# Shifted places in SBUF for activations and split weights of a decoder step, with one ring skipped per MLP chunk

## The chip, the cores and the metric

The kernel runs on one core of one Trainium2 chip. The metric is the time of one execution on the device, in microseconds (us): the median of three runs of the kernel before was 2753.49 us (2752.89 to 2754.78). The profile is of one further execution.

## The reference

The reference is one inference step of a two-layer decoder on 320 tokens: 256 of a prompt and 8 x 8 of samples. Width is 2048. Layer 0 mixes tokens by gated linear attention (four heads, chunks of 64, a carried state), layer 1 by a gated MLP over positions (chunks of 128). Each layer ends with a dense MLP of inner width 8192. Residuals are scaled and normalised:

```python
def sq_relu_mlp(x, w1, w2):
    return jnp.square(jax.nn.relu(x @ w1)) @ w2
...
h, s = gla_mixer(x, ...)          # layer 0;  sg_mixer(x, ...) in layer 1
x = layer_norm(DEEPNORM_ALPHA * x + h, ln1_g[i], ln1_b[i])
x = layer_norm(DEEPNORM_ALPHA * x + sq_relu_mlp(x, mlp_w1[i], mlp_w2[i]), ln2_g[i], ln2_b[i])
```

All inputs and outputs are float32. The outputs are both groups' activations, both new attention states, and the normalised v rows of layer 1.

## The kernel before, in words

Activations are kept transposed: 128 features on the partitions, 16 k tiles of T = 320 tokens along the free dimension, so one k tile is 1,280 bytes in each partition. Weights are the stationary operand, activations stream. To keep float32 accuracy with the faster fp32r type, every operand is split into a high part, rounded to fp32r, and a low part, the rest. `mm3` (lines 149 to 154) makes one product of three matmuls into the same PSUM tile: low weights with high activations (line 152), high weights with low activations (153), high with high (154). They are 17,664 of the kernel's matmuls.

Weights come in units (`unit`, lines 130 to 143): four k tiles by 256 output columns. A unit is a DMA of 512 KB from the SP queue into one of three `raw` buffers, a cast on ScalarE into the high tile (line 141) and a subtraction on VectorE into the low tile (line 142). TensorE then does 24 matmuls on it: two column halves, four k tiles, three products. `group` (line 156) walks over the four units (q = 0 to 3) of one block of 256 output columns, so the k tile is 4 q plus the tile in the unit; `gemm`, `gemm_of` and `residual_gemm` walk over the blocks. A GEMM of 2048 x 2048 is 32 units or 768 matmuls.

High and low tiles stand in rings (`Ring`, lines 47 to 58). A ring has two buffers of 4,096 bytes for the high part, a gap, two for the low part, and a second gap that fills up to 256 bytes (LINE = 64 floats). High tiles start at a multiple of 256 bytes; low tiles lie the gap beyond one. `next_ring` takes the rings in turn: "a" and "c" from the start, in the attention; "b" and "d" as well, once `second_half` (line 625) has freed space, during the output projection of layer 0. So from there on the four units of a group always meet the same four rings in the same order.

Activation tiles have a spare of 64 floats (BIG, line 35), and `bigtile` (line 189) may begin inside it. PLACES (line 37) gives these starts, in floats, for the high and low part, for each MLP: four pairs for the hidden tiles (hh, hl) of the four chunks of the MLP, one for its input y (yh, yl), and one for other tiles (the input of `sg_w_in` from the first row, ph and pl, the input of `sg_w_out`, from the second). The tiles of x, o and dg begin at 0. dg is the residual before its normalisation, with two further columns (TW = 322): the first group of a GEMM reads it while the normalisation is still being worked out, and `correct` mends the result.

An MLP (`mlp`, line 799) goes in four chunks of 2048 inner columns. Each is a w1 GEMM, whose results are squared and split into hh and hl on their way out of PSUM (lines 811 to 813), and a w2 GEMM, whose results are added to z. The order on each engine comes from the tile framework's planner, which follows the order of the program text and the readiness of operands; TensorE's order is that of the loops above.

Of the kernel before, what the change touches and what calls it, by code (L numbers as in the profile page):

```python
# [20 lines left out]
T = TP + DB * DS  # L21
# [12 lines left out]
LINE = 64  # L34
BIG = KT * T + LINE

PLACES = [[(0, 0), (16, 16), (32, 32), (48, 48), (0, 16), (16, 32)],
          [(32, 48), (48, 0), (0, 48), (16, 0), (32, 16), (48, 32)]]


V_BG, V_NG = 0, 8
# [5 lines left out]
class Ring:  # L47
# [5 lines left out]
    def part(self, p, name):  # L53

        t = self.pool.tile([P, UK, UN], F32R, tag=p + self.tag, name=name)
        if self.gap:
            self.pool.tile([P, self.gap.pop(0)], F32, tag=f"gap{p}{self.tag}", name=name + "_gap", bufs=1)
        return t


class Side:
# [17 lines left out]
def step_kernel(ctx: ExitStack, tc: tile.TileContext, A):  # L79
# [3 lines left out]
    def nm(s):  # L83
        uid[0] += 1
        return f"{s}_{uid[0]}"
# [5 lines left out]
    wa = ctx.enter_context(tc.tile_pool(name="wa", bufs=2))  # L91
# [2 lines left out]
    gl = gls.enter_context(tc.tile_pool(name="gl", bufs=4, space=bass.MemoryType.PSUM))  # L94
    mx = None

    rings = [Ring(wa, "a", 32), Ring(wa, "c", 48)]
    turn = [0]
    banks = [0]
    units = [0]  # L100
# [25 lines left out]
    def col(c):  # L126
        return vec[:, c : c + 1]
# [17 lines left out]
    def next_ring():  # L145
        turn[0] += 1
        return rings[turn[0] % len(rings)]
# [38 lines left out]
    w_in = A["gla_w_in"]  # L186
    C_Q, C_K, C_V, C_R = 0, H * DK, 2 * H * DK, 2 * H * DK + H * DV

    def bigtile(tag, dt, name, width=T, start=0):

        t = (lp if tag == "b1" else big).tile([P, BIG], dt, tag=tag, name=nm(name))
        return t[:, start : start + KT * width].rearrange("p (k t) -> p k t", t=width)

    def parts(pair, name, width=T, starts=(0, 0)):
        return (bigtile(pair + "0", F32R, name + "h", width, starts[0]),
                bigtile(pair + "1", F32R, name + "l", width, starts[1]))

    xh, xl = parts("a", "x")
    o_all = bigtile("b0", F32, "o_all")

    gst = ExitStack()
# [104 lines left out]
    class Head:  # L306


        def __init__(hd, h):
            hd.h = h  # L310
            hd.eb, hd.ei, hd.ee = {}, {}, {}
# [304 lines left out]


    oh, ol = parts("a", "o")

    def split_o(ks):  # L620
        for k in ks:
            nc.scalar.copy(oh[:, k, 0:T], o_all[:, k, 0:T])
            nc.vector.tensor_sub(ol[:, k, 0:T], o_all[:, k, 0:T], oh[:, k, 0:T].bitcast(F32))

    def second_half():

        nonlocal lp, l2, z, gl, mx
        side.flush()
        split_o(range(4 * (H - 1), 4 * H))
        gst.close()  # L630
        gls.close()
        gl = ctx.enter_context(tc.tile_pool(name="gs", bufs=2, space=bass.MemoryType.PSUM))
        mx = ctx.enter_context(tc.tile_pool(name="mx", bufs=2, space=bass.MemoryType.PSUM))
        banks[0] = 3
        lp = ctx.enter_context(tc.tile_pool(name="lp", bufs=1))
        l2 = ctx.enter_context(tc.tile_pool(name="l2", bufs=2))
        wb = ctx.enter_context(tc.tile_pool(name="wb", bufs=2))
        rings.extend((Ring(wb, "b", 8), Ring(wb, "d", 40)))
        wb.tile([P, LINE // 4], F32, tag="fill", name="fill_b", bufs=1)
        z = lp.tile([P, KT, T], F32, tag="z", name="z")  # L640
        lp.tile([P, LINE], F32, tag="fill", name="fill_l")
        for q in range(2):
            nc.gpsimd.dma_start(z[:, 8 * q : 8 * q + 8, :], xT[:, 8 * q : 8 * q + 8, :])
# [113 lines left out]
    def gemm(w, row0, col0, rh, rl, evict, quad=False, side=None, before=None):  # L757

        i = 0
        while i < D // UN:  # L760
            n2 = 2 if quad and i == 0 else 1
            group(w, row0, [col0 + (i + m) * UN for m in range(n2)], rh, rl,
                  lambda n, ps, i=i: evict(2 * i + n, ps), side, before=before if i == 0 else None)
            i += n2

    def gemm_of(norm, out, w, col0, evict_raw, evict, starts):

        yh, yl = parts(out, "y", starts=starts)
        norm.close()
        side = Side([lambda j=j: norm.apply(j, yh, yl) for j in range(KT)], 3 * NU)  # L770
        group(w, 0, (col0, col0 + UN), *norm.raw, evict_raw, side, width=TW)
        side.flush()
        for i in range(2, D // UN):
            group(w, 0, (col0 + i * UN,), yh, yl, lambda n, ps, i=i: evict(2 * i + n, ps))
        return yh, yl

    def residual_gemm(w, rh, rl, row0, scale, vg, vb, raw, quad=False, side=None, before=None, last=False):

        norm = None

        def evict(j, ps):
            nonlocal norm
            if j == 0:
                norm = Norm(z, vg, vb, raw, last)
            zj = z[:, j, :]
            if j < KT // 2:
                nc.vector.scalar_tensor_tensor(zj, zj, scale, ps[:], op0=ALU.mult, op1=ALU.add)
            else:
                nc.vector.tensor_add(zj, zj, ps[:])
            norm.add(j)  # L790
            if j == KT // 2 - 1:
                for i in range(KT // 2, KT):
                    zi = z[:, i, :]
                    nc.vector.scalar_tensor_tensor(zi, zi, scale, norm.c[:], op0=ALU.mult, op1=ALU.subtract)

        gemm(w, row0, 0, rh, rl, evict, quad, side, before)
        return norm

    def mlp(i, norm, y_in, h_in, vg, vb, raw, last=False):

        w1, w2 = A["mlp_w1"][i], A["mlp_w2"][i]
        NC_ = 4
        for c in range(NC_):
            hs = []

            def sq_relu(j, x, r):
                if not hs:
                    hs.extend(parts(h_in, "h", starts=PLACES[i][c]))
                hh, hl = hs
                f = l2.tile([P, T], F32, tag="f", name=nm("f"))  # L810
                nc.vector.scalar_tensor_tensor(f[:], x, 0.0, r[:], op0=ALU.max, op1=ALU.mult)
                nc.scalar.copy(hh[:, j, 0:T], f[:])
                nc.vector.tensor_sub(hl[:, j, 0:T], f[:], hh[:, j, 0:T].bitcast(F32))

            def evict(j, ps):
                r = l2.tile([P, T], F32, tag="r", name=nm("r"))
                nc.scalar.activation(r[:], ps[:], AF.Relu)
                sq_relu(j, ps[:], r)

            def evict_raw(j, ps):  # L820
                t, wb_ = norm.correct(ps)
                r = l2.tile([P, T], F32, tag="r", name=nm("r"))
                nc.scalar.activation(r[:], t[:], AF.Relu, bias=wb_)
                sq_relu(j, r[:], r)

            if c == 0:
                yh, yl = gemm_of(norm, y_in, w1, 0, evict_raw, evict, PLACES[i][4])
            else:
                gemm(w1, 0, c * D, yh, yl, evict)
            if c < NC_ - 1:  # L830
                def evz(j, ps, s=ALPHA if c == 0 else 1.0):
                    nc.vector.scalar_tensor_tensor(z[:, j, :], z[:, j, :], s, ps[:], op0=ALU.mult, op1=ALU.add)
                gemm(w2, c * D, 0, *hs, evz)
            else:
                return residual_gemm(w2, *hs, c * D, 1.0, vg, vb, raw, last=last)
# [4 lines left out]
    def before(q):  # L840
        if q == NU - 1:
            second_half()

    norm = residual_gemm(A["gla_w_out"], oh, ol, 0, ALPHA, V_L1G, V_L1B, "b", quad=True,
                         side=side, before=before)
    norm = mlp(0, norm, "a", "b", V_L2G, V_L2B, "a")


# [21 lines left out]
    def put_v(j, x, bias):  # L870
        nonlocal v, nv
        if j == 0:
            v = bigtile("a0", F32, "v")
            nv = Norm(v, V_SG, V_SBB)
        vj = v[:, j, 0:T]
        nc.scalar.activation(vj, x, AF.Gelu, bias=bias)
        if j >= KT // 2:
            nc.vector.tensor_sub(vj, vj, nv.c[:])
        nv.add(j)
        if j == 3:  # L880
            spatial()

    def ev_v_raw(j, ps):
# [5 lines left out]
    yh, yl = gemm_of(norm, "b", A["sg_w_in"], D, ev_v_raw, lambda j, ps: put_v(j, ps[:], col(V_SB + KT + j)),  # L889
                     PLACES[0][5])  # L890

# [43 lines left out]
    gemm(A["sg_w_in"], 0, 0, yh, yl, ev_u, side=side)  # L935
    ph, pl = parts("b", "p", starts=PLACES[1][5])
    for k in range(KT):
        nc.scalar.copy(ph[:, k, 0:T], v[:, k, 0:T])
        nc.vector.tensor_sub(pl[:, k, 0:T], v[:, k, 0:T], ph[:, k, 0:T].bitcast(F32))

    norm = residual_gemm(A["sg_w_out"], ph, pl, 0, ALPHA, V_L1G + KT, V_L1B + KT, "a", quad=True)
    norm = mlp(1, norm, "b", "a", V_L2G + KT, V_L2B + KT, "b", last=True)


# [20 lines left out]
    for j in range(KT):  # L965
        y, g, b = z[:, j, :], col(norm.vg + j), col(norm.vb + j)
        if j in on_pool:
            t = l2.tile([P, T], F32, tag="s", name=nm("t"))
# [3 lines left out]
        else:  # L972
            if j not in ps:
                put_d(j)
            t = l2.tile([P, T], F32, tag="t", name=nm("t"), bufs=3)
# [70 lines left out]
```

## Time and profile before

| What | Value |
|---|---|
| Median of the runs (lowest, highest) | 2753.49 us (2752.89, 2754.78) |
| The profiled execution's own time | 2754.99 us |
| Its span, first to last instruction | 2753.3 us |
| Mean granted TensorE clock | 0.998 |
| HBM read, written | 409.60 MB, 22.02 MB |
| DMA over the span | 157 GB/s |

The span lies 1.7 us below the execution's own time. In the page, PE is TensorE's matmuls, PEld its weight loads, DVE VectorE, ACT ScalarE, POOL GpSimd, SP the engine that issues most DMAs; "busy" is the time in which at least one instruction of the engine runs. A matmul's recorded duration runs from its start to its modelled end and overlaps the next one's, so a mean of 309 ns doesn't mean that one begins every 309 ns. In a row of a group, "x768 | 242.5, 316 | 10.1" is the count, the busy time in us, the mean duration in ns and the idle time of the engine before them. In a row of a stretch, the count in brackets takes in all instructions that overlap the stretch.

### The profile page before, as it was taken

The numbers are of one execution on the slowest core, as the hardware profiler recorded it, in microseconds if no ns is written. First come the engines' busy times: TensorE is split into PE (matmuls) and PEld (weight loads), VectorE is DVE, ScalarE is ACT, GpSimd is POOL, SyncE is SP. The second block draws the span as 40 slices with busy tenths as digits, with TensorE's granted clock in tenths as the row PEclk, the third lists the DMA queues.
The fourth block names the chain that finished last, engine by engine and source line by source line (L and its number), as shares of the span: only waits on it lengthen the run. The fifth ranks groups of instructions, "written<-read, shape, count | busy, mean of one in ns | idle before, by whom it ended". The sixth has DMA issues, their size and how long they took to land.

```text
span 2753.3 us, 44617 instructions
## 1 busy us (share of the span) xinstructions
PE 2728.7 (99%) x18493; PEld 2705.0 (98%) x18493; DVE 1546.0 (56%) x2284; ACT 1185.3 (43%) x1698; POOL 54.6 (2%) x84
## 2 busy tenths in 40 slices
PE   8999999999999999999999999999999999999998
PEld 8999998999999999999999999999999999999998
DVE  6567577785444444444468764686444444444446
ACT  5545455464334334333446554455334323323434
POOL 1000000000000000000001000000000000000001
PEclk9999999999999999999999999999999999999999
DMA  6557566645444444444445444454444444444442
GB/s 223 178 194 233 174 201 207 199 140 160 149 150 152 148 152 147 152 149 150 151 142 169 153 138 131 138 159 152 150 151 148 153 147 152 149 150 148 151 147 75
DMA packets 126396, 434.52 MB, mean 158 GB/s; under 512 B 13681, under 2 KB 17905, under 8 KB 126193
## 3 DMA queue, kind: packets, MB, share of 16 engines
q1 hardware_dynamic: 118800, 407.29, 47.5%
q0 software_dynamic: 6512, 23.20, 2.5%
q8 instruction: 144, 2.36, 0.3%
q10 hardware_dynamic: 880, 1.18, 0.1%
q14 instruction: 60, 0.48, 0.0%
HBM read 409.60 MB, written 22.02 MB: 157 GB/s over the span
## 4 chain that ended last, share of the span: by engine, by line
PE 97%; DVE 1%; DMA 1%; ACT 1%; issue 0%; SPq 0%; ACTq 0%; DVEq 0%
PE mm L154 31%; PE mm L152 31%; PE mm L153 31%; PE gl L564 1%; PE gl L567 1%; PE gl L522 0%; PE gl L905 0%; PE gl L506 0%; DMA xr<-xT 0%; DMA raw<-gla_w_out 0%; DMA raw<-gla_w_in 0%; ACT z L979 0%; PE gl L900 0%; ACT wh L141 0%; DVE wl L142 0%
## 5 line engine op out<-in xcount | busy, mean ns | idle before, releaser
L142 DVE TENSOR_TENSOR wl<-raw,wh 128x1024 fp32r<-128x1024 f32 (+1 forms) x738 | 901.9, 1223 | 967.3 <-ACT wh L141 964.6
L141 ACT CAST wh<-raw 128x1024 fp32r<-128x1024 f32 (+1 forms) x738 | 773.4, 1049 | 1234.6 <-PE mm L154 1124.6
L154 PE MATMUL mm<-yh,wh 128*128 128x320 f32 x2368 | 731.9, 310 | 0.0
L153 PE MATMUL mm<-yl,wh 128*128 128x320 f32 x2368 | 730.5, 309 | 0.0
L152 PE MATMUL mm<-yh,wl 128*128 128x320 f32 x2368 | 726.3, 309 | 0.0
L154 PE MATMUL mm<-hh,wh 128*128 128x320 f32 x2048 | 632.5, 309 | 0.0
L153 PE MATMUL mm<-hl,wh 128*128 128x320 f32 x2048 | 632.4, 309 | 0.0
L152 PE MATMUL mm<-hh,wl 128*128 128x320 f32 x2048 | 631.4, 308 | 0.0
L154 PEld LDWEIGHTS mm<-yh,wh 128*128 128x128 f32 x2368 | 445.2, 188 | 0.0
L153 PEld LDWEIGHTS mm<-yl,wh 128*128 128x128 f32 x2368 | 444.8, 188 | 0.0
L152 PEld LDWEIGHTS mm<-yh,wl 128*128 128x128 f32 x2368 | 443.6, 188 | 0.0
L153 PEld LDWEIGHTS mm<-hl,wh 128*128 128x128 f32 x2048 | 384.8, 188 | 0.0
L152 PEld LDWEIGHTS mm<-hh,wl 128*128 128x128 f32 x2048 | 384.5, 188 | 0.0
L154 PEld LDWEIGHTS mm<-hh,wh 128*128 128x128 f32 x2048 | 384.4, 188 | 0.0
L152 PE MATMUL mm<-xh,wl 128*128 128x320 f32 x768 | 242.5, 316 | 10.1 <-ACT xh L215 5.6
L153 PE MATMUL mm<-xl,wh 128*128 128x320 f32 x768 | 238.7, 311 | 0.0
L154 PE MATMUL mm<-xh,wh 128*128 128x320 f32 x768 | 238.6, 311 | 0.0
L152 PEld LDWEIGHTS mm<-xh,wl 128*128 128x128 f32 x768 | 145.5, 190 | 15.0 <-ACT xh L215 5.6
L153 PEld LDWEIGHTS mm<-xl,wh 128*128 128x128 f32 x768 | 145.7, 190 | 3.6 <-issue 1.2
L154 PEld LDWEIGHTS mm<-xh,wh 128*128 128x128 f32 x768 | 145.6, 190 | 1.3
L152 PE MATMUL mm<-oh,wl 128*128 128x320 f32 x256 | 79.2, 313 | 4.8 <-DVE nw L178 4.8
L153 PE MATMUL mm<-ol,wh 128*128 128x320 f32 x256 | 79.8, 313 | 0.0
(271 smaller groups left out, 2475.4 us busy)
## 6 DMA issues: line engine op xcount, KB each, us to landing
raw<-mlp_w SPq DMA_DIRECT2D x512, 512.0 KB, 3.5
raw<-gla_w_in SPq DMA_DIRECT2D x94, 512.0 KB, 3.9
raw<-sg_w_in SPq DMA_DIRECT2D x64, 512.0 KB, 3.6
st<-state SPq DMA_DIRECT2D x32, 512.0 KB, 4.1
o_state_s<-st POOLq DMA_DIRECT2D x32, 512.0 KB, 3.9
raw<-gla_w_out SPq DMA_DIRECT2D x32, 512.0 KB, 4.1
raw<-sg_w_out SPq DMA_DIRECT2D x32, 512.0 KB, 3.5
z<-xT POOLq DMA_DIRECT2D x2, 1280.0 KB, 10.5
```

The lines of the kernel that those rows point to most:

```text
L141: nc.scalar.copy(hi[:, ks, :], raw[:, ks, :])
L142: nc.vector.tensor_sub(lo[:, ks, :], raw[:, ks, :], hi[:, ks, :].bitcast(F32))
L152: nc.tensor.matmul(ps, wl[:, kk, s], x_h, start=first, stop=False)
L153: nc.tensor.matmul(ps, wh[:, kk, s], x_l, start=False, stop=False)
L154: nc.tensor.matmul(ps, wh[:, kk, s], x_h, start=False, stop=last)
L564: nc.tensor.matmul(po[:], qm[:, kt, b * P : (b + 1) * P], part[:], start=False, stop=(b == DB - 1 and kt == 1 and part is sth))
L567: nc.tensor.matmul(pu[:], kz[:, g, i, kt * P : (kt + 1) * P], hd.vts[:, g, :], start=True, stop=True)
```

## The change

Three things change, all of them addresses or the choice of a buffer.

1. Hidden, y and p tiles are reached through a new class `Rows`. Tile k begins at `start + k*T + 4*(k//2)` floats: every second tile, the offset grows by 16 bytes, to 112 bytes at the last two. The high and low part do so alike. Tiles without a start in PLACES (x, o, dg, v) are as before.
2. PLACES: hidden tiles of all four chunks start at 0 and 0 in the first MLP, at 32 and 32 floats in the second. Starts of y and of the input of `sg_w_in` stay; p goes from (48, 32) to (32, 0).
3. The gap between high and low weights becomes 16, 24, 32 and 8 floats in rings a, c, b and d (64, 96, 128 and 32 bytes; before 128, 192, 32 and 160). At each MLP chunk `next_ring()` is called once more, so one ring is passed over, and units meet the rings shifted by one.

```diff
-PLACES = [[(0, 0), (16, 16), (32, 32), (48, 48), (0, 16), (16, 32)],
-          [(32, 48), (48, 0), (0, 48), (16, 0), (32, 16), (48, 32)]]
+PLACES = [[(0, 0)] * 4 + [(0, 16), (16, 32)], [(32, 32)] * 4 + [(32, 16), (32, 0)]]
...
+class Rows:
+    def __init__(self, buf, start):
+        self.buf, self.start = buf, start
+
+    def __getitem__(self, key):
+        p, k, t = key
+        at = self.start + k * T + 4 * (k // 2)
+        return self.buf[p, at + t.start : at + t.stop]
...
-    rings = [Ring(wa, "a", 32), Ring(wa, "c", 48)]
+    rings = [Ring(wa, "a", 16), Ring(wa, "c", 24)]
...
-    def bigtile(tag, dt, name, width=T, start=0):
+    def bigtile(tag, dt, name, width=T, start=None):
 
         t = (lp if tag == "b1" else big).tile([P, BIG], dt, tag=tag, name=nm(name))
+        if start is not None:
+            return Rows(t, start)
+        start = 0
         return t[:, start : start + KT * width].rearrange("p (k t) -> p k t", t=width)
 
-    def parts(pair, name, width=T, starts=(0, 0)):
+    def parts(pair, name, width=T, starts=(None, None)):
...
-        rings.extend((Ring(wb, "b", 8), Ring(wb, "d", 40)))
+        rings.extend((Ring(wb, "b", 32), Ring(wb, "d", 8)))
...
         for c in range(NC_):
             hs = []
+            next_ring()
```

## The prediction

> **What bounds the kernel now.** I read the page's busy times first, then the chain that ended last, then the costliest groups.
>
> ```profile
> PE 2728.7 (99%) x18493; PEld 2705.0 (98%) x18493; DVE 1546.0 (56%) x2284; ACT 1185.3 (43%) x1698; POOL 54.6 (2%) x84
> ...
> PE 97%; DVE 1%; DMA 1%; ACT 1%; issue 0%; SPq 0%; ACTq 0%; DVEq 0%
> PE mm L154 31%; PE mm L152 31%; PE mm L153 31%; PE gl L564 1%; PE gl L567 1%; PE gl L522 0%; PE gl L905 0%; PE gl L506 0%; DMA xr<-xT 0%; DMA raw<-gla_w_out 0%; DMA raw<-gla_w_in 0%; ACT z L979 0%; PE gl L900 0%; ACT wh L141 0%; DVE wl L142 0%
> ...
> L142 DVE TENSOR_TENSOR wl<-raw,wh 128x1024 fp32r<-128x1024 f32 (+1 forms) x738 | 901.9, 1223 | 967.3 <-ACT wh L141 964.6
> L141 ACT CAST wh<-raw 128x1024 fp32r<-128x1024 f32 (+1 forms) x738 | 773.4, 1049 | 1234.6 <-PE mm L154 1124.6
> ...
> raw<-mlp_w SPq DMA_DIRECT2D x512, 512.0 KB, 3.5
> ```
>
> TensorE never stops: the three matmuls of mm3 (lines 152 to 154) are 93% of the chain. Casting and splitting the weights is not late; ACT sits idle 1124.6 us before its casts because TensorE has not yet given a weight buffer back. So only the pitch of the matmuls (start to start) counts. 736 units of 24 matmuls make 17,664 of them, so 1 ns of pitch is 17.7 us.
>
> A matmul's duration overlaps the next one's. The timeline shows the pitch, and what runs beside it.
>
> ```profile
> 1000.05 0.30 PE L152 MATMUL mm<-hh,wl 128*128 128x320 f32 x1
> 1000.05 0.19 PEld L153 LDWEIGHTS mm<-hl,wh 128*128 128x128 f32 x1
> 1000.19 0.31 PE L153 MATMUL mm<-hl,wh 128*128 128x320 f32 x1
> 1000.19 0.19 PEld L154 LDWEIGHTS mm<-hh,wh 128*128 128x128 f32 x1
> ```
>
> The load of the next weights begins with each matmul and reads SBUF while the activations stream. Where these two reads lie to each other is all that the change touches, so I ask whether the pitch depends on place. Below are stretches of 110 us, each inside one GEMM of 768 equal matmuls: time, then each engine's busy time with its instruction count. First the four w2 GEMMs of the first MLP (hh, hl), then four of the second, then three w1 GEMMs of the first MLP (yh, yl), three of the second, last sg_w_out (ph, pl).
>
> ```profile
> core 0: us, PE busy (x) PEld busy (x) DVE busy (x) ACT busy (x) POOL busy (x), PEclk, DMA share, GB/s
> ...
> 686.00:796.00 110.00, 110.00 (x754) 110.00 (x753) 45.45 (x49) 34.27 (x34) 0.00 (x0) 1.00 0.49 151
> 912.00:1022.00 110.00, 110.00 (x757) 110.00 (x756) 46.09 (x49) 33.41 (x33) 0.00 (x0) 1.00 0.49 152
> 1137.00:1247.00 110.00, 110.00 (x752) 110.00 (x751) 45.60 (x47) 33.18 (x33) 0.00 (x0) 1.00 0.49 151
> 1362.00:1472.00 110.00, 110.00 (x753) 110.00 (x752) 71.52 (x113) 46.34 (x63) 0.00 (x0) 1.00 0.48 151
> 1944.00:2054.00 110.00, 110.00 (x752) 110.00 (x751) 45.30 (x48) 34.23 (x34) 0.00 (x0) 1.00 0.47 150
> 2170.00:2280.00 110.00, 110.00 (x757) 110.00 (x756) 46.04 (x48) 33.76 (x33) 0.00 (x0) 1.00 0.49 152
> 2395.00:2505.00 110.00, 110.00 (x746) 110.00 (x745) 44.64 (x47) 33.32 (x33) 0.00 (x0) 1.00 0.48 149
> 2621.00:2731.00 110.00, 110.00 (x748) 110.00 (x747) 64.12 (x106) 38.55 (x58) 0.00 (x0) 1.00 0.36 110
> ...
> 800.00:910.00 110.00, 110.00 (x751) 110.00 (x750) 51.71 (x61) 44.17 (x60) 0.00 (x0) 1.00 0.49 149
> 1025.00:1135.00 110.00, 110.00 (x750) 110.00 (x750) 51.70 (x61) 44.18 (x60) 0.00 (x0) 1.00 0.47 149
> 1250.00:1360.00 110.00, 110.00 (x751) 110.00 (x751) 51.68 (x61) 44.15 (x60) 0.00 (x0) 1.00 0.48 150
> 2057.00:2167.00 110.00, 110.00 (x752) 110.00 (x751) 51.23 (x61) 44.33 (x60) 0.00 (x0) 1.00 0.48 151
> 2283.00:2393.00 110.00, 110.00 (x752) 110.00 (x751) 51.81 (x61) 44.11 (x60) 0.00 (x0) 1.00 0.49 149
> 2508.00:2618.00 110.00, 110.00 (x752) 110.00 (x751) 51.23 (x61) 44.34 (x60) 0.00 (x0) 1.00 0.48 151
> ...
> 1719.00:1829.00 110.00, 110.00 (x750) 110.00 (x749) 75.83 (x123) 49.62 (x74) 0.00 (x0) 1.00 0.48 149
> ```
>
> About two matmuls of each count were begun before the stretch, so the pitch is 110.00 over the count less 2. The clock is 1.00 throughout and TensorE full, yet the GEMMs differ: 145.7 ns (x757) to 147.8 ns (x746). Rows with equal places repeat within one matmul (the w1 rows). So place matters, by about 2 ns between best and worst.
>
> **What the change does to each stage.** By stage, with L the distance of low weights behind high ones modulo 256 bytes, and h and l the offsets of the activations' two parts:
>
> Second-half stages now use L = 128, 192, 32 and 160 in turn; afterwards 64, 96, 128 and 32. Tiles of 1,280 bytes keep one offset modulo 256 through a GEMM now; afterwards it moves by 16 bytes every second k tile, from 0 to 112 over sixteen tiles. The first MLP's hidden tiles start at h = l = 0, 64, 128, 192 in its four chunks, later always at 0. The second MLP's start at (128, 192), (192, 0), (0, 192), (64, 0), later always at (128, 128). The y tiles keep their starts; p goes from (192, 128) to (128, 0). No matmul, load or byte is added.
>
> The nearest row for a moving offset is the normalised activations dg, whose tiles are 322 columns wide, so that each k tile lies 8 bytes further modulo 256, with h = l.
>
> ```profile
> L152 PE MATMUL mm<-dgh,wl x64: 304/310/316, 572.2 to 600.7; 128*128 128x322 f32 x64
> ```
>
> From first to last are 63 triples and four statistics matmuls (lines 679 and 680): 28.5 us / 193 = 147.7 ns, and by 320/322 for the wider tile 146.8 ns. A moving offset thus gives neither the best nor the worst row but the middle, and starts off every 32-byte border cost nothing to speak of. I take 146.8 ns for every stage that moves. The ends are the best and worst row, 145.7 and 147.8.
>
> The sum, from the pitches in the rows:
> - First MLP, w2: 3,072 matmuls, rows 754, 757, 752, 753, mean 110/752 = 146.3. To 146.8: +1.6 us. This stage loses, because equal fixed offsets do better than the middle.
> - Second MLP, w2: 3,072, rows 752, 757, 746, 748, mean 110/748.75 = 146.9: -0.3 us.
> - w1, first MLP: 2,880 at 110/748.67 = 146.9: -0.4 us. Second: 2,880 at 110/750 = 146.7: +0.4 us. sg_w_in: 1,344, whose offsets keep their starts too, taken at 146.8: 0.
> - sg_w_out: 768 at 110/748 = 147.1: -0.2 us.
> - The first half, where the x tiles don't move but L does (rings a and c, 128 and 192 to 64 and 96):
>
> ```profile
> 174.70:186.70 12.00, 12.00 (x85) 12.00 (x84) 4.69 (x6) 5.09 (x9) 0.00 (x0) 1.00 0.49 156
> ...
> 174.58 0.31 PE L153 MATMUL mm<-xl,wh 128*128 128x320 f32 x1
> ...
> 186.67 0.30 PE L152 MATMUL mm<-xh,wl 128*128 128x320 f32 x1
> ```
>
> From 174.58 to 186.67 lie 83 matmuls (85 less 2): 145.7 ns, as good as the best row. This place is given up for two that no row shows. 2,304 matmuls, and some 384 of gla_w_out before the other rings open: nothing if the new pair is as good, +1.1 ns or 3.0 us if it is middling, +2.1 ns or 5.6 us if it is as the worst row. I take half of the middling loss, +1.5 us, as equal zero offsets did well in the row x754 too.
> - dg itself: 576 matmuls, new L only, taken at 0; between best and worst row ±0.6 us.
> - Evictions that now write at 16-byte offsets: no such write is in the trace but dg's; the casts and subtractions of h are these.
>
> ```profile
> L813 DVE TENSOR_TENSOR hl<-f,hh 128x320 fp32r<-128x320 f32 x128 | 62.5, 488 | 29.5 <-ACT hh L812 29.5
> L812 ACT CAST hh<-f 128x320 fp32r<-128x320 f32 x128 | 58.8, 459 | 32.4 <-DVE f L811 32.4
> ```
>
> They lie beside matmuls on engines 56% and 43% busy; doubled, they would still be hidden: 0.
> - The skipped ring at each chunk's start: four rings of two buffers give some seven units of 3.5 us (24 x 146.8 ns) ahead, six or so after a skip. Load 3.5, cast 1.0 and subtraction 1.2 us fit in: 0. Without that cover the eight skips would cost 5.7 us each, 46 us.
>
> Together +2.6 us. The profiled execution took 2754.99 us (span 2753.3 and 1.7 around it) and so comes to 2757.6; the median shown is 1.5 us lower, so I predict **2756 us**. Bounds of the moving stages: 14,016 matmuls at the best row's 145.7 instead of 146.7 are -14 us, at the worst row's 147.8 +15 us; an average over sixteen meetings of q and L per stage should stay well inside, at a third of that.
>
> **The rivals.** (1) *The new places are good.* For it: the rows x757 (twice) and the x stage show 145.7 is to be had, and hidden tiles with h = l do better than unequal ones (146.3 against 146.9). Against: dg moves with h = l and is middling. If the moving stages reach 145.7 throughout, -14 us: 2739; halfway with the x stage unchanged, 2747.
>
> (2) *Slower: the moving offset keeps meeting badly.* If each shift sets the two reads to collide anew, before the stream has settled, the moving stages go towards the row x746, +1.1 ns on 14,016: +15 us, and with the first half's loss of 3.0 us 2772; halfway 2763. The second MLP's hidden row x746 shows such a pitch through a whole GEMM. It counts from a mean pitch 0.3 ns above today's, on all 17,664. Against it: dg again, within 0.1 ns of the mean.
>
> (3) *Place does nothing*, as two reads through separate ports would have it: then 2753.5 stays. The Trainium skill states this on the page SBUF — State Buffer (section SBUF: two separate sides): TensorE never waits on anyone at SBUF, each door being its own; the page TensorE: Matmul & The Clock Gate (section What happens when you issue a matmul) gives the streamed operand and the weights a read port each. By that rule all terms above are 0. The rows speak against it: equal work in 110 us, x746 to x757, with the clock at 1.00.
>
> **How the numbers follow.** A measurement here can tell about 0.2%, 5.5 us: faster is below 2748, slower above 2759. Middling places, 55%: within 0.2%, apart from a part above when the first half loses its full 3 to 5.6 us. Good places 17%: faster. Bad places 25%: slower. No effect 3%. Giving the edges of the middle case to both sides: faster 0.18, same 0.54, slower 0.28. The middle's own range is 2749 to 2762; with the halfway points of both rivals 2746 to 2766.
>
> **What would show it.** In the profile after: the same 110 us inside the GEMMs give counts of 749 to 752 for hidden, y and p stages alike, the spread between chunks smaller than x746 to x757 because each chunk now passes through eight offsets; dg's 64 triples still take 28.5 us; a clean x stretch of 83 matmuls takes 12.1 to 12.3 us. TensorE stays at 99% and ACT's idle time before line 141 is still ended by TensorE. I am wrong if the hidden stages stand at 755 or more (rival 1) or 747 and less (rival 2), or if TensorE waits for line 142 at chunk starts.

## The result and the profile after

The changed kernel takes 2758.14 us (median of 20 runs, 2756.06 to 2760.09), the kernel before 2753.52 us (20 runs, 2752.55 to 2755.77): a ratio of 1.0015 with a 95% interval of 1.0008 to 1.0022. It is slower, by less than the 0.2% that I had called the border. The forecast was 2756 us, within 0.2%, in a range of 2746 to 2766.

The profiled execution took 2757.38 us with a span of 2755.6 us, 2.4 us more than the profiled one of before; the medians lie 4.6 us apart, because the profile of before was 1.5 us above its kernel's median and this one 0.8 us below. The page after, busy times and chain (mm3's lines are now 163 to 165):

```profile
PE 2731.7 (99%) x18493; PEld 2707.9 (98%) x18493; DVE 1543.0 (56%) x2284; ACT 1183.0 (43%) x1698; POOL 54.1 (2%) x84
...
PE mm L163 31%; PE mm L165 31%; PE mm L164 31%; PE gl L578 1%; PE gl L581 1%; PE gl L536 0%; DMA raw<-gla_w_out 0%; DMA xr<-xT 0%; PE gl L920 0%; PE gl L520 0%; DVE wl L153 0%; DMA raw<-gla_w_in 0%; ACT z L994 0%; PE gl L915 0%; DVE ol L637 0%
...
L152 ACT CAST wh<-raw 128x1024 fp32r<-128x1024 f32 (+1 forms) x738 | 771.6, 1047 | 1231.8 <-PE mm L165 1091.6
```

TensorE is as full as before, and the casts still wait for it: the skipped rings leave no weight late. The stretches of 110 us after, with the columns of those shown of before; four w2 GEMMs of the first MLP, four of the second, three w1 GEMMs of each, then sg_w_out:

```profile
686.00:796.00 110.00, 110.00 (x753) 110.00 (x752) 44.11 (x47) 32.35 (x32) 0.00 (x0) 1.00 0.47 147
912.00:1022.00 110.00, 110.00 (x753) 110.00 (x752) 44.62 (x47) 31.93 (x32) 0.00 (x0) 1.00 0.47 144
1137.00:1247.00 110.00, 110.00 (x751) 110.00 (x751) 44.30 (x46) 31.89 (x32) 0.00 (x0) 1.00 0.46 145
1362.00:1472.00 110.00, 110.00 (x753) 110.00 (x752) 71.56 (x112) 45.89 (x63) 0.00 (x0) 1.00 0.49 151
1946.00:2056.00 110.00, 110.00 (x750) 110.00 (x750) 43.90 (x46) 32.14 (x32) 0.00 (x0) 1.00 0.48 146
2172.00:2282.00 110.00, 110.00 (x748) 110.00 (x747) 43.47 (x47) 32.43 (x32) 0.00 (x0) 1.00 0.48 146
2398.00:2508.00 110.00, 110.00 (x751) 110.00 (x750) 43.86 (x46) 32.30 (x32) 0.00 (x0) 1.00 0.48 147
2624.00:2734.00 110.00, 110.00 (x748) 110.00 (x748) 63.72 (x105) 38.01 (x58) 0.00 (x0) 1.00 0.35 108
799.00:909.00 110.00, 110.00 (x752) 110.00 (x751) 52.09 (x61) 43.97 (x60) 0.00 (x0) 1.00 0.50 155
1024.00:1134.00 110.00, 110.00 (x751) 110.00 (x750) 52.17 (x61) 43.74 (x60) 0.00 (x0) 1.00 0.51 156
1250.00:1360.00 110.00, 110.00 (x753) 110.00 (x752) 52.04 (x61) 44.03 (x60) 0.00 (x0) 1.00 0.50 154
2059.00:2169.00 110.00, 110.00 (x747) 110.00 (x747) 51.52 (x61) 43.58 (x59) 0.00 (x0) 1.00 0.50 154
2286.00:2396.00 110.00, 110.00 (x751) 110.00 (x751) 52.03 (x61) 44.00 (x60) 0.00 (x0) 1.00 0.50 154
2511.00:2621.00 110.00, 110.00 (x749) 110.00 (x748) 51.62 (x61) 43.61 (x59) 0.00 (x0) 1.00 0.50 155
1720.00:1830.00 110.00, 110.00 (x752) 110.00 (x752) 74.84 (x123) 48.58 (x74) 0.00 (x0) 1.00 0.47 144
```

Before, hidden chunks lay between x746 and x757; now between x748 and x753. They have drawn together, around 146.5 ns in the first MLP and 147.1 in the second. The forecast of 749 to 752 for hidden, y and p rows was too narrow: eight of the fifteen lie in it, the others at 747, 748 and 753. The dg row and the clean x stretch after:

```profile
L163 PE MATMUL mm<-dgh,wl x64: 304/312/317, 571.2 to 599.9; 128*128 128x322 f32 x64
```

```profile
174.06 0.31 PE L164 MATMUL mm<-xl,wh 128*128 128x320 f32 x1
...
186.36 0.31 PE L164 MATMUL mm<-xl,wh 128*128 128x320 f32 x1
```

dg takes 28.7 us instead of 28.5. The x stretch has 28 triples (the three matmuls of one `mm3`) in 12.30 us, 146.4 ns; it was 145.7.

### The profile page after: what moved, and what is told of

It reads as the page before. It is cut to its first block, busy times and chain, and to the rows that moved or that the text cites. A ratio compares the mean times of both kernels' runs of the same rounds, so it can differ in the third digit from the quotient of the medians.

```text
span 2755.6 us, 44595 instructions
## 1 busy us (share of the span) xinstructions
PE 2731.7 (99%) x18493; PEld 2707.9 (98%) x18493; DVE 1543.0 (56%) x2284; ACT 1183.0 (43%) x1698; POOL 54.1 (2%) x84
## 4 chain that ended last, share of the span: by engine, by line
PE 97%; DMA 1%; DVE 1%; ACT 0%; issue 0%; SPq 0%; ACTq 0%; DVEq 0%
PE mm L163 31%; PE mm L165 31%; PE mm L164 31%; PE gl L578 1%; PE gl L581 1%; PE gl L536 0%; DMA raw<-gla_w_out 0%; DMA xr<-xT 0%; PE gl L920 0%; PE gl L520 0%; DVE wl L153 0%; DMA raw<-gla_w_in 0%; ACT z L994 0%; PE gl L915 0%; DVE ol L637 0%
## 5 line engine op out<-in xcount | busy, mean ns | idle before, releaser
L163 PE MATMUL mm<-ph,wl 128*128 128x320 f32 x256 | 78.9, 310 | 1.0 <-ACT ph L953 1.0
```

Of the source, the lines that this page charges most:

```text
L163: nc.tensor.matmul(ps, wl[:, kk, s], x_h, start=first, stop=False)
```

## The experiments

"Count" is TensorE's in a 110 us stretch inside one GEMM. 764 means 144.4 ns a matmul, 758 145.5, 752 146.7, 747 147.7, 730 151.1.

### The parts by themselves

First the gaps alone, and the moving tiles with their starts alone.

```diff
 # e1_gaps: the kernel before with
-    rings = [Ring(wa, "a", 32), Ring(wa, "c", 48)]
+    rings = [Ring(wa, "a", 16), Ring(wa, "c", 24)]
-        rings.extend((Ring(wb, "b", 8), Ring(wb, "d", 40)))
+        rings.extend((Ring(wb, "b", 32), Ring(wb, "d", 8)))
```

> Only the new gaps between high and low weights (64, 96, 128, 32 bytes); activations at their old fixed places, no ring skipped. Theory (pitch is set by the distances of the two reads modulo 256 bytes; moving offsets give the middle): the first half loses what it lost in the changed kernel, x from a mean of 145.9 to 146.4 ns, and every hidden and y stage gets another fixed place and so another pitch between 145.7 and 147.8 ns, with a spread between chunks as wide as before: 2750 to 2760 us. Rival A (the gaps alone made the loss): 2758 us. Rival B (place does nothing, the loss is elsewhere): 2753.5 us with the same counts per stretch as before.

Measured: 2749.97 us (2747.86 to 2752.26) beside 2754.21 of before, ratio 0.9985 (0.9976 to 0.9995): faster, by 0.15%, and at the lower edge of what was expected. The stretches of a hidden chunk (first MLP) and of a y GEMM (second MLP):

```profile
912.00:1022.00 110.00, 110.00 (x758) 110.00 (x758) 46.08 (x48) 32.79 (x32) 0.00 (x0) 1.00 0.47 149
...
2057.00:2167.00 110.00, 110.00 (x758) 110.00 (x757) 51.98 (x62) 44.77 (x62) 0.00 (x0) 1.00 0.48 149
```

The second is where most of the gain comes from: y of the second MLP was x752, and its 2,880 matmuls take 3.2 us less in this trace than in that of before, of the 4.2 us by which the medians differ. The x stage lost what was expected, 145.9 to 146.4 ns in the mean. So the new gaps are not what makes the changed kernel slower; rivals A and B fall.

```diff
 # e2_moving: the changed kernel with the old gaps and without the skipped ring
-    rings = [Ring(wa, "a", 16), Ring(wa, "c", 24)]
+    rings = [Ring(wa, "a", 32), Ring(wa, "c", 48)]
-        rings.extend((Ring(wb, "b", 32), Ring(wb, "d", 8)))
+        rings.extend((Ring(wb, "b", 8), Ring(wb, "d", 40)))
-            next_ring()
```

> Only the moving k tiles with their new starts; old gaps, no ring skipped. Theory: the x stage keeps its 145.9 ns; the hidden chunks of both MLPs draw together to 146.3 to 147.2 ns from a spread of 145.8 to 147.9; y stages 146.6 to 147.3: 2753 to 2759 us. Rival A (the gaps alone made the loss): 2753.5 us. Rival B (place does nothing): the hidden chunks keep their old counts.

Measured: 2753.89 us (2753.0 to 2755.75), ratio 0.9998 (0.9989 to 1.0008): no difference. Hidden chunks, two of each MLP:

```profile
686.00:796.00 110.00, 110.00 (x751) 110.00 (x751) 45.22 (x48) 32.56 (x31) 0.00 (x0) 1.00 0.47 149
912.00:1022.00 110.00, 110.00 (x751) 110.00 (x751) 45.08 (x47) 33.36 (x32) 0.00 (x0) 1.00 0.49 151
...
2170.00:2280.00 110.00, 110.00 (x750) 110.00 (x750) 44.94 (x47) 32.86 (x32) 0.00 (x0) 1.00 0.48 149
2396.00:2506.00 110.00, 110.00 (x750) 110.00 (x749) 44.97 (x47) 32.89 (x32) 0.00 (x0) 1.00 0.48 150
```

Good chunks (x757) and bad ones (x746) have both gone to the middle. The middle isn't one figure, though: the y GEMMs of the first MLP stand at 146.2 to 146.3 ns here, lower than the 146.6 to 147.3 expected, those of the second at 147.2. And the parts don't add: -4.2 us and -0.3 us alone, +4.6 us together. The next two runs ask what joins them.

```diff
 # e5_no_skip: the changed kernel without
-            next_ring()
 # e6_still: the changed kernel with
-        at = self.start + k * T + 4 * (k // 2)
+        at = self.start + k * T
```

> The changed kernel without the skipped ring; gaps and moving places stay. Theory (moving gives the middle, the skip only changes which ring meets which k tiles): hidden chunks of one MLP, which differed in the changed kernel by up to 0.5 ns, become equal within 0.1 ns, at 146.3 to 147.3 ns; y chunks too; 2754 to 2761 us. Rival (the skip is what joins gaps and moving into a loss): 2749 to 2751 us, the sum of the two single changes.

Measured: 2757.16 us in one run beside 2753.76, as slow as the changed kernel. The three hidden chunks of an MLP that were counted are now the same within one: x752, x753, x752 in the first, x749, x749, x748 in the second. Without the skip the parts still don't add; it is not what joins them.

> The changed kernel with the k tiles held still: new starts, new gaps and the skipped ring stay. Theory (the fixed places were good with the new gaps, and moving took that away): hidden tiles at (0, 0) and (128, 128) as the same places with the new gaps in the run with the gaps alone, 146.1 ns, y of the second MLP 145.6 ns: 2746 to 2752 us. Rival (gaps and skip, or the new starts, are to blame): 2756 to 2760 us.

Measured: 2747.27 us (2746.39 to 2750.39), ratio 0.9977 (0.9968 to 0.9987). A hidden chunk and a y GEMM of the second MLP:

```profile
912.00:1022.00 110.00, 110.00 (x755) 110.00 (x754) 44.13 (x48) 33.05 (x32) 0.00 (x0) 1.00 0.46 145
...
2057.00:2167.00 110.00, 110.00 (x757) 110.00 (x756) 53.13 (x63) 45.74 (x64) 0.00 (x0) 1.00 0.49 154
```

Held still, the changed kernel is faster than the one before, by 0.23%. All of its loss, and more, is the 16-byte steps: 2758.1 to 2747.3, some 11 us. The new gaps gain while the places are fixed (4.2 us in e1_gaps) and lose where they move (2757.2 in e5_no_skip against 2753.9 in e2_moving), and that is why the parts don't add.

### Does a place have a price of its own?

I took the best distances that a unit of the kernel before had shown (144.5 ns) and the worst (148.4, late in the unit 151) and gave them to all stages but dg.

```diff
 # e3_good: the kernel before with
+PLACES = [[(48, 0)] * 6, [(48, 0)] * 6]
+    rings = [Ring(wa, "a", 32), Ring(wa, "c", 32)]
+        rings.extend((Ring(wb, "b", 32), Ring(wb, "d", 32)))
+    xh, xl = parts("a", "x", starts=(48, 0))
+    oh, ol = parts("a", "o", starts=(48, 0))
 # e4_bad: the same lines with (16, 0) for (48, 0) and 48 for 32
```

> All low weights 128 bytes beyond the high ones, all activations fixed at 192 bytes (high) and 0 (low), x and o too; only dg stays as it is. In the kernel before, the units with these distances took 144.5 ns a matmul. Theory: all stages but dg at about 144.5 ns, 2.1 ns less on some 17,000 matmuls: 2715 to 2722 us. Rival B (what differs between the chunks is not the place but their data, buffers or neighbours): 2750 to 2757 us. Rival C (place matters, but a good place is good only after the units of the other rings): 2730 to 2745 us.

> All low weights 192 bytes beyond the high ones, all activations fixed at 64 bytes (high) and 0 (low). In the kernel before, the units with these distances took 148.4 ns a matmul, and 151 ns towards their end. Theory: 148.4 to 151 ns in all stages but dg: 2783 to 2825 us. Rival B (not the place): 2750 to 2757 us. Rival C (a place is bad only after the units of other rings): 2755 to 2775 us.

Measured: e4_bad 2822.09 us (2821.52 to 2822.69), ratio 1.0246 (1.0229 to 1.0264), as forecast. A stretch counts x730, which is 151.1 ns, and in the timeline line 153 comes round after 0.45 us; in the trace's nanoseconds the same three pitches, 150, 147 and 157, follow each other over and over:

```profile
686.00:796.00 110.00, 110.00 (x730) 110.00 (x729) 44.74 (x47) 33.53 (x35) 0.00 (x0) 1.00 0.47 148
...
1000.05 0.31 PE L153 MATMUL mm<-hh,wh 128*128 128x320 f32 x1
1000.20 0.31 PE L151 MATMUL mm<-hh,wl 128*128 128x320 f32 x1
1000.35 0.32 PE L152 MATMUL mm<-hl,wh 128*128 128x320 f32 x1
1000.50 0.31 PE L153 MATMUL mm<-hh,wh 128*128 128x320 f32 x1
```

So addresses alone move the time by 2.5%, and rival 3 of the prediction, place does nothing, is out. Writes of the other engines aren't what the matmuls meet: of the 255 triples of the first MLP's second hidden chunk, the 202 that run beside an instruction of VectorE or ScalarE and the 53 that don't all take 453 or 454 ns.

But e3_good missed: 2749.80 us (2747.84 to 2751.61), ratio 0.9984 (0.9975 to 0.9994), where I had expected 2715 to 2722. Two stretches of 50 us of it, in sg_w_out and across the border of a w2 and a w1 GEMM, show why. Distances, matmuls and clock are the same:

```profile
1772.00:1822.00 50.00, 50.00 (x348) 50.00 (x347) 43.42 (x77) 27.13 (x44) 0.00 (x0) 1.00 0.48 154
1000.00:1050.00 50.00, 50.00 (x343) 50.00 (x342) 21.16 (x23) 17.18 (x20) 0.00 (x0) 1.00 0.47 148
```

50 us over 346 and over 341 matmuls are 144.5 and 146.6 ns. Unit by unit, wherever the pitch of e3_good stays the same for many units running and no other matmul comes between, it is one of three values, 144.5, 145.5 and 146.7 ns. My theory, one pitch per place, falls. The new one: the weight load and the stream settle into a repeating pattern; at one place several patterns are stable; the phase in which a stage is entered picks one, and it stays until something shifts the phase. Its rival was that the MLP stages have a reason of their own for 146.7.

### Shifting the phase

```diff
 # e8_kicks: e3_good, and in group, before the first matmul of a block of 256 columns
+                if kick and q == 0 and i == 0:
+                    nc.tensor.matmul(ps[0][:, 0:kick], wl[:, 0, 0:P], rl[:, 0, 0:kick], start=True, stop=True)
 # at the first and fifth block of twelve GEMMs, kick = 288, 290, ... 302
```

> The kernel with the good fixed places (128; 192 and 0), with one further short matmul of 288 to 302 columns before the first and fifth block of twelve GEMMs, 24 in all, whose result is overwritten at once. In the run without them the same places stood at 146.7 ns in the MLPs but at 144.5 and 145.5 ns in o, sg_w_in and p. Theory (several patterns are stable at one place, and the phase at which a stage is entered picks one, which then stays): the short matmul shifts the phase, and after some of the 24 the pitch stands at 144.5 or 145.5 ns until the next one: 2728 to 2747 us. Rival (the MLP stages run at 146.7 ns for a reason of their own, such as their traffic): 146.7 ns throughout, 2751 to 2755 us.

Measured: 2741.98 us in one run beside 2753.76. First a stretch of e3_good, at the place of the first two half GEMMs, 146.7 ns; then from this run the eight half GEMMs behind the first eight short matmuls, 54 us each:

```profile
686.00:796.00 110.00, 110.00 (x752) 110.00 (x751) 45.84 (x48) 32.53 (x31) 0.00 (x0) 1.00 0.47 149
...
686.00:740.00 54.00, 54.00 (x376) 54.00 (x375) 23.25 (x25) 16.78 (x17) 0.00 (x0) 1.00 0.48 154
741.50:795.50 54.00, 54.00 (x376) 54.00 (x375) 22.49 (x23) 16.14 (x16) 0.00 (x0) 1.00 0.50 155
797.00:851.00 54.00, 54.00 (x373) 54.00 (x373) 24.77 (x28) 21.20 (x29) 0.00 (x0) 1.00 0.47 155
853.00:907.00 54.00, 54.00 (x376) 54.00 (x375) 26.07 (x31) 22.19 (x30) 0.00 (x0) 1.00 0.49 155
909.00:963.00 54.00, 54.00 (x370) 54.00 (x369) 22.44 (x24) 16.62 (x17) 0.00 (x0) 1.00 0.47 153
965.00:1019.00 54.00, 54.00 (x376) 54.00 (x375) 22.31 (x24) 16.34 (x16) 0.00 (x0) 1.00 0.49 155
1021.00:1075.00 54.00, 54.00 (x370) 54.00 (x370) 24.71 (x28) 20.79 (x29) 0.00 (x0) 1.00 0.48 152
1077.50:1131.50 54.00, 54.00 (x376) 54.00 (x375) 26.07 (x31) 21.82 (x30) 0.00 (x0) 1.00 0.50 153
```

One matmul of 0.13 us changes the next 384 from 146.7 to 144.5 ns (x370, x376), or from 144.5 to 145.5 (x373), and the other way. Against e3_good nothing but the short matmuls was added, and in e3_good these GEMMs all stand at 146.7. That the MLPs have a reason of their own is out. What follows isn't chance either: in 15 of the 24 cases a width met the same pattern as another short matmul of that width, and each time the same pattern followed. 298 columns led from 146.7 to 144.5 three times, 300 from 144.5 to 146.7 twice, and 290 twice left 146.7 as it was. So it is the width that matters, not merely that one matmul is added.

Do moving tiles have lasting patterns? The changed kernel with the same 24 short matmuls, and the bad places with moving tiles:

```diff
 # e10_kicks_moving: the changed kernel with the short matmuls of e8_kicks
 # e7_bad_moving: e4_bad, with Rows (16 bytes every other k tile) for the y, h and p tiles
```

> The changed kernel with the 24 short matmuls of the earlier run. They cost 3.2 us themselves. Theory (with moving tiles no pattern lasts, so a shifted phase is forgotten): the hidden and y stages keep the pitch of the changed kernel within 0.3 ns: 2758 to 2764 us. Rival (moving tiles have lasting patterns too): single half GEMMs fall or rise by 1 ns and more, 2745 to 2775 us.

Measured: 2763.82 us in one run beside 2753.41. Four half GEMMs behind short matmuls of 288, 290, 292 and 294 columns:

```profile
686.00:740.00 54.00, 54.00 (x371) 54.00 (x370) 22.51 (x25) 17.17 (x19) 0.00 (x0) 1.00 0.49 148
741.50:795.50 54.00, 54.00 (x371) 54.00 (x370) 21.03 (x23) 14.71 (x14) 0.00 (x0) 1.00 0.45 137
798.00:852.00 54.00, 54.00 (x370) 54.00 (x369) 26.23 (x31) 21.54 (x28) 0.00 (x0) 1.00 0.51 157
855.00:909.00 54.00, 54.00 (x370) 54.00 (x370) 25.78 (x31) 21.64 (x30) 0.00 (x0) 1.00 0.49 147
```

In both traces, with and without the short matmuls, the mean pitch of each half GEMM agrees within 0.13 ns, and from the fifth unit behind a short matmul on each unit agrees within 0.04 ns. Where tiles move, a shift of phase is forgotten within four units, that is within one pass over the sixteen k tiles. (Of the 6.4 us over the changed kernel's profile 3.2 are the short matmuls; 1.8 arose in the first 573 us, before any of them, and 1.3 behind the last GEMM.)

> The kernel with the bad fixed places (192; 64 and 0), whose y, h and p tiles now move by 16 bytes every other k tile; x and o keep the bad places. Theory (fixed places lock the two reads into one repeating pattern, good or bad, and a moving offset breaks the lock and gives the middle): y, h and p stages fall from 151.1 to 146.5 to 147.5 ns, x and o stay slow by some 8 us: 2758 to 2770 us. Rival (a place has its own cost, and moving averages the costs of the places passed, of which the first are bad): 148 to 150 ns, 2780 to 2810 us.

Measured: 2765.15 us (2764.43 to 2765.32), ratio 1.0039 (1.0024 to 1.0054), 57 us less than with the bad places fixed. Twelve of the sixteen y and hidden GEMMs stand at 146.7 ns, three of the others, which begin behind dg or end before it, at 146.9 or 147.0, and the last one, which other matmuls break up, at 147.8; the first hidden chunk:

```profile
686.00:796.00 110.00, 110.00 (x752) 110.00 (x751) 46.71 (x50) 34.13 (x35) 0.00 (x0) 1.00 0.48 150
```

Moving is thus neither good nor bad in itself: it costs 11 us where the fixed places are good (e6_still against the changed kernel) and saves 57 where they are bad.

### Only distances?

```diff
 # e11_shifted: e4_bad with 64 bytes ahead of the rings, and (32, 16) for (16, 0)
+    wa.tile([P, 16], F32, tag="front", name="front_a", bufs=1)
...
+        wb.tile([P, 16], F32, tag="front", name="front_b", bufs=1)
```

(A filler behind the first rings keeps the other tiles where they were.)

> The kernel with the bad fixed places, with everything that TensorE reads, high and low weights and both parts of the activations, 64 bytes further on. Theory (only the distances between the reads count): 151.1 ns as before the shift, 2818 to 2826 us. Rival (the addresses themselves count, say by a fixed slot for each): another pitch, 144.5 to 150 ns, 2740 to 2805 us.

Measured: 2820.95 us in one run; the stretch counts x730 as in e4_bad:

```profile
686.00:796.00 110.00, 110.00 (x730) 110.00 (x729) 45.15 (x48) 33.08 (x34) 0.00 (x0) 1.00 0.48 146
```

Only dg was not shifted. A common shift of 64 bytes changes nothing here: it is the distances that count. Another shift, or one of the good places, was not tried.

### A faster kernel

If a pattern lasts, one short matmul per MLP should do. It comes first at the fifth block of the first w1 GEMM, then, in the last run, at the start of the first w2 GEMM, where e3_good stands at 146.7.

```diff
 # e9_locked: e3_good with the short matmul in gemm_of only
+                  kick=kick if i == 4 else 0)      # 298 columns, 296 in sg_w_in
 # e12_once: e3_good with it in gemm only, for the w2 GEMM of chunk 0
+                  kick=298 if kicks and i == 0 else 0)
```

> The good fixed places with one short matmul of 298 columns at the fifth block of the first w1 GEMM of each MLP (296 in sg_w_in), three in all. In the run with 24 of them, 298 columns led from 146.7 to 144.5 ns each of three times. Theory (the pattern entered stays until something shifts the phase): 144.5 ns from there through all chunks of the MLP, some 10,700 matmuls 2.2 ns shorter than without: 2722 to 2732 us. Rival (a pattern holds for one block of units and is lost at GEMM borders): 2740 to 2749 us.

Measured: 2737.43 us (2735.86 to 2737.71), ratio 0.9940 (0.9923 to 0.9956). It beat the stated rival but missed the stated time: the pattern entered was 145.5 ns, not 144.5, and it stood from there through all GEMM borders of both MLPs (x758, x757 and x758 in three hidden chunks). In the trace the short matmul ran earlier than the program has it, in the fourth block: behind 148 of the y matmuls instead of 192. There e3_good stands at 145.7 ns and has not settled at 146.7 yet, so I take it that the same shift started from another phase.

> The good fixed places with one short matmul of 298 columns per MLP, at the start of its first w2 GEMM, where without it the pattern of 146.7 ns has settled. Three times before, 298 columns led from 146.7 to 144.5 ns. Theory (the pattern that is left and the shift decide the next one, which then stays over GEMM borders): 144.5 ns from there to the last w2 GEMM of each MLP, some 10,000 matmuls 2.2 ns shorter than the 2749.8 us without: 2724 to 2733 us. Rival (the pattern that follows is chance, or GEMM borders change it): 145.5 or 146.7 ns in one MLP or both, 2735 to 2751 us.

Measured: 2726.95 us (2726.22 to 2727.2), ratio 0.9902 (0.9886 to 0.9919). Two hidden chunks of the first MLP:

```profile
686.00:796.00 110.00, 110.00 (x764) 110.00 (x763) 46.03 (x49) 33.60 (x32) 0.00 (x0) 1.00 0.50 153
909.00:1019.00 110.00, 110.00 (x764) 110.00 (x763) 46.32 (x48) 33.24 (x32) 0.00 (x0) 1.00 0.49 153
```

It beats both kernels, by 26.0 us and by 31.2: the same places as e3_good, and two matmuls more.

## Why the prediction was right, point by point

**The bound.** Right: TensorE stayed at 99%, and only the pitch changed. The skipped rings, the 16-byte writes and the casts cost nothing that the profile shows, as forecast: from the last matmul before a chunk to its first, the trace has 144 to 151 ns, an ordinary pitch.

**The sum.** Measured as the difference of the two traces, from the first to the last matmul of each GEMM:

| Term | Forecast, us | Measured, us |
|---|---|---|
| First MLP, w2 | +1.6 | +0.9 |
| Second MLP, w2 | -0.3 | +0.5 |
| First MLP, w1 | -0.4 | -0.3 |
| Second MLP, w1 | +0.4 | +1.4 |
| sg_w_in | 0 | +0.9 |
| sg_w_out | -0.2 | -0.4 |
| First half (x and gla_w_out) | +1.5 | -0.8 (see below) |
| dg | 0 | +0.3 |
| Together | +2.6 | +2.5 |

That the last row agrees is luck. Its first-half term can't be read from one pair of traces: e1_gaps, e5_no_skip, e6_still and e10_kicks_moving have the places of the changed kernel up to the end of gla_w_out, and in these five traces the half takes anything from 564.5 to 567.1 us, because its waits differ from one execution to the next. The pitch doesn't differ: in the x stage, neighbouring matmuls follow each other after 145.9 ns in the kernel before and after 146.4 to 146.5 in all five. Some 2,090 of them make +1.2 us, close to the +1.5 forecast; in gla_w_out the pitch stays at 146.2 to 146.3. The other rows together are +3.3 us where the forecast has +1.1. With the 1.2 that is +4.5, and the medians differ by 4.6. So the forecast of +2.6 was 2 us short, inside its range.

The step that carried the forecast, that every stage that moves goes to the middle, as dg shows, held: in the changed kernel these stages lie between 146.4 and 147.6 ns (the last GEMM, which other matmuls break up, aside), in e2_moving between 146.2 and 147.3, in e7_bad_moving between 146.7 and 147.1. "This stage loses, because equal fixed offsets do better than the middle" held as well, and e6_still measures it: 146.1 ns fixed, 146.4 to 146.8 moving in the first MLP.

What was mis-sized is the one figure of 146.8 for all moving stages: the middle is not the same for all gaps and starts. sg_w_in and the second MLP's w1 went to 147.4 and 147.2 ns, together 2 us more than forecast.

**What the prediction had not seen.** It asked what a place costs. Its rival 1, good places, took a row's 145.7 ns as a price that other stages could be given; e3_good, whose places had shown 144.5, stood at 146.7 in most stages. The prediction came out right because the moving tiles make the question idle: e10_kicks_moving shows that with them no pattern lasts. Its small difference is also the sum of two larger things that it did not name, -6.5 us (the new gaps and starts, by e6_still against its kernel before) and some +11 us (the steps of 16 bytes); it needed neither, as it went from the old rows straight to the middle.

**The rule weighed.** The rule of rival 3, that no address matters, would have left the time unchanged in every run; instead the pitch is 151.1 ns in e4_bad and 144.5 in e12_once, with the same instructions but two. By the Trainium skill (page SBUF — State Buffer, section SBUF: two separate sides) TensorE never waits on anyone at SBUF. The traces don't contradict this as far as other engines go; that the two reads of TensorE itself leave each other alone, as rival 3 took it, doesn't fit them.

What stays open: which part of the chip the weight load and the stream share, why a step of 16 bytes per two k tiles forgets the pattern, and whether a smaller or larger step would. That the two reads collide is argued from the distances and from the load's place beside the stream; no run took one of the reads away. Four of the runs (e5_no_skip, e8_kicks, e10_kicks_moving, e11_shifted) are single executions; their readings rest mainly on counts inside the trace.

## What to carry to other kernels

When TensorE is full and every matmul loads new weights, compare the count of matmuls in equal stretches of equal work: if it differs, the distance in SBUF between weights and streamed operand is worth trying, and the time of one stage is no price of that place before it has been seen from several entering phases. Don't add up such changes measured singly: gaps alone gained 4.2 us, moving tiles alone nothing, both together lost 4.6. Where a good pattern is stable, a single short matmul at the right spot may lock it in, as in e12_once; where none can be found, moving the tiles is insurance against a bad one, as in e7_bad_moving.

## What the runs showed of the hardware that I had not expected

The steady pitches at one place are few and evenly spaced: 144.45, 145.55 and 146.67 ns, 1.1 ns apart, and 151.1 at the other places of e4_bad is four such steps further on. A pattern lasts: in e12_once 144.5 ns held from 683 us on through every unit of six whole GEMMs and half of a seventh, some 5,000 matmuls in each MLP, across changes of PSUM tile, weight ring and activation tile. It ended where one other matmul (line 721, a sum for the normalisation) comes between; behind it stood 145.5. In e9_locked the pattern of 145.5 changed to 144.5 at the same matmul. Patterns also repeat: e3_good's trace has the same sequence of unit pitches after dg in both MLPs. And one matmul of 0.13 us, whose result is thrown away, is worth about 11 us for each MLP behind it (22.9 us for two, 2749.8 to 2726.95).
